# Two decoder layers on one core: the norm of queries and keys is cut into token blocks, and the steps of the attention chains are spaced anew

## The chip, the cores and the metric

The kernel runs on one core of a Trainium2 chip. The metric is the device time of one execution in microseconds, the median over runs. Five engines work side by side, each in the order of its own queue: TensorE (PE in the profile; its weight loads stand apart as PEld), VectorE (DVE), ScalarE (ACT), GpSimd (POOL) and SyncE (SP), which here issues nearly all DMAs. An instruction that has to wait holds up everything behind it in its queue.

## The reference

Input are 256 tokens of 2048 numbers, in float32. Two layers follow each other, each a mixer and an MLP around one residual stream:

```python
h = rms_norm(x, mix_norm_g[i])
x = x + (fox_attention(h, ...) if i == 0 else dilated_attention(h, ...))
h = rms_norm(x, mlp_norm_g[i])
x = x + (relu(h @ w_up) ** 2) @ w_down          # 2048 -> 8192 -> 2048
```

FoX attention (layer 0) has 16 heads of 128. One matrix gives queries, keys, values and a forget gate; queries and keys are normed per head (`q * rsqrt(mean(q*q) + eps) * gain`); the logits get the difference of the gate's cumulative log-sigmoid and a causal mask; softmax, product with the values, output matrix.

Dilated attention (layer 1) has 8 heads whose values are 256 wide, shared by three groups of dilations 1, 4 and 16. Each group has its own queries and keys, normed in the same way, a distance bias and a window; the three groups share one softmax denominator.

## The kernel before, in words

**Float32 by halves.** Every float32 operand is cut into a high half in the fast matmul format and a low half, the remainder. A product of 128 rows (`product_steps`, lines 369 to 371) is three matmuls for each of two token blocks: high x high, high x low, low x high. So each weight block of 256 rows x 512 columns, loaded by SP into `raw` (line 315), is split by `split`: ScalarE casts `wh` (L334), VectorE subtracts `wl` (L335). There are five buffers of `raw` and five of `wh` and `wl`. Each new load waits until the block just split has been read.

**Steps.** Products of 16 row blocks (`KC`) by 512 columns follow each other in a fixed order: four groups of query, key and value columns for FoX, its output matrix, the first MLP, four groups for the dilated layer (three times queries and keys, then values), its output matrix, the second MLP. One row block is one step: six matmuls, then `jobs.tick()`. At odd steps a weight block is used up and the next is split.

**Jobs.** Everything else is written as Python generators that run between the steps. `yield 3` means: go on three steps later; `yield ("fk", j)` means: go on when that key is done. This is settled while the program is built, by counting steps, not on the chip. From step 24 on `pin` fixes the order of each engine's instructions as written, so a job that is set one step later stands behind that step's work in every queue.

**The jobs that the change touches.** `qk_chain` (L544) norms the queries and keys of one product: ScalarE squares both token blocks of the accumulators (L550), VectorE sums (L554), GpSimd takes the power -0.5 (L557); three steps later VectorE multiplies by it (L563, `qn`) and turns 32x32 blocks (L572) for both token blocks in one go, and SP writes them to a scratch in DRAM (`blocks`, through `move`, L291); four steps later SP reads them back turned; six steps later ScalarE applies the gains and casts (L589, L596), and VectorE takes the low halves (L600). `transposed_by_dma` (L459) does the same for the normed input of an MLP or of the dilated layer: transpose (L466), block writes, 3 steps, read-back, 6 steps, scaling (L485, L487).

`fox_head` and `dil_head` then take the scores (`scores`, L680 and L683, into the two banks of `ps_sc`), maximum, exponential and sum, turn the probabilities by way of DRAM (`p_turned`), cast and cut them (`p_split`: `pTh` L657, two steps on `pTl` L660) and multiply them with the values (`pv`, L630 and L631). `pv` casts the result (`oTfh`, `oTdh`, L633) and takes the low half (`oTfl`, `oTdl`, L635) for the output matrix.

`in_group` runs the first three chunks of the output matrix as one group: rows 0 to 11 of all chunks first, then rows 12 to 15 of each, since the last heads come late (`CUT = 12`). When a chunk is done, `add_chain` adds it to the residual (L876) and starts the norm of that chunk. The first two chunks of an up-projection and the first two products of the dilated layer are grouped in the same way.

Tiles live in pools by tag; `bufs` says how many of a tag exist. The tag `w` holds the squares, the normed queries and keys, and the turned inputs; `sd` the three score blocks of a dilated head; `vw` a value block; `pTh` and `pTl` the probabilities.

Of the kernel before, what the change touches and what calls it, by code (L numbers as in the profile page):

```python
# [9 lines left out]
F32 = mybir.dt.float32  # L10
F32R = mybir.dt.float32r
I32 = mybir.dt.int32
AF = mybir.ActivationFunctionType
# [4 lines left out]
P = 128  # L18
# [20 lines left out]
CUT = 12  # L39
# [52 lines left out]
def trunk(ctx: ExitStack, tc, x, fox_w_in, fox_b_f, fox_q_gain, fox_k_gain, fox_w_out, dil_w_in,  # L92
# [3 lines left out]
    pinned = {"last": None}  # L96

# [146 lines left out]
    def add_group(*chunks):  # L244

        for rows in ((0, CUT * P), (CUT * P, D)):
            for w, cols in chunks:
                add(w, rows, cols)

    def add_out(w):  # L250
        add_group(*((w, [(n * NC, NC)]) for n in range(3)))
        for n in range(3, NX):
            add(w, (0, D), [(n * NC, NC)])
# [34 lines left out]
    def move(dst, src):  # L288

        with behind(issued["load"]):  # L290
            return nc.sync.dma_start(dst, src)  # L291
# [167 lines left out]
    def transposed_by_dma(tag, col, n):  # L459


        tiles = []
        for t in range(NT):
            tile_ = work.tile([P, NC], F32, tag="w", name=f"turned_{tag}_{n}_{t}", bufs=5)
            blocks = dram.tile([4, 32, 4, P], F32, tag="blocks", name=f"blocks_{tag}_{n}_{t}", bufs=4)
            nc.vector.transpose(tile_.rearrange("p (j b r) -> p b j r", j=4, b=4),  # L466
                                xt[n][:, t, :].rearrange("p (b j c) -> p b j c", j=4, c=32))
            for i in range(4):
                move(blocks[:, :, i, :].rearrange("j c x -> c j x"),
                     tile_[32 * i:32 * i + 32].rearrange("p (j x) -> p j x", j=4))  # L470
            tiles.append((tile_, blocks))
        yield 3
        for tile_, blocks in tiles:
            move(tile_, blocks.rearrange("j c i x -> (j c) (i x)"))
        yield 6
        for half in range(2):
            pr = n * 2 + half
            both = act.tile([P, 2, 2, S], F32R, tag="hT", name=f"hT_{tag}_{pr}", bufs=KC // 2)
            for i in range(2):
                gc = gain[:, col + pr * 2 + i:col + pr * 2 + i + 1]  # L480
                for t in range(NT):
                    src = tiles[t][0].rearrange("p (i b r) -> p b i r", i=4, b=4)[:, half * 2 + i]
                    hi, lo = (both[:, i, x, t * P:(t + 1) * P].rearrange("p (i r) -> p i r", i=4) for x in range(2))
                    with behind(issued["cast"]):
                        on_act = nc.scalar.activation(hi, src, AF.Copy, scale=gc)  # L485
                    with behind(issued["cut"]):
                        on_dve = nc.vector.scalar_tensor_tensor(lo, src, gc, hi.bitcast(F32), ALU.mult, ALU.subtract)  # L487
            issued[tag, pr] = issued[tag] = on_act, on_dve
            hT[tag][pr] = both
            jobs.done.add((tag, pr))  # L490
            yield 1

    def norm_chain(tag, col, n, ssp, wait, later):
# [24 lines left out]
        with behind(issued["cast"]):  # L518
            for t in range(NT):
                junk = work.tile([P, 3 * 3 * P], F32, tag="sd", name=f"junk_{tag}_{n}_{t}", bufs=1)  # L520
                nc.scalar.activation(junk[:, 0:NC], xt[n][:, t, :], AF.Square, accum_out=ssp[:, t, n:n + 1])
# [22 lines left out]
    def qk_chain(acc, tag, key, parts):  # L544
# [3 lines left out]
        for t in range(NT):  # L548
            s = work.tile([P, NC], F32, tag="w", name=f"sq_{key}_{t}", bufs=5)
            nc.scalar.activation(halves(s), by_column(acc[t]), AF.Square, scale=rstd[tag][:, t:t + 1])  # L550
            sq.append(s)
# [6 lines left out]
        yield 3  # L558
        qn = []
        for t in range(NT):  # L560
            nc.vector.tensor_scalar_mul(rq[:, t, :], rq[:, t, :], rstd[tag][:, t:t + 1])
            q = work.tile([P, 4, P], F32, tag="w", name=f"qn_{key}_{t}", bufs=5)
            nc.vector.tensor_mul(q.rearrange("p (h g) d -> p h g d", h=2),  # L563
                                 acc[t].rearrange("p (g d h) -> p h g d", h=2, g=2),
                                 rq[:, t, :].rearrange("p (h g) -> p h g", h=2).unsqueeze(3).to_broadcast([P, 2, 2, P]))
            qn.append(q)


        turns = []
        for t in range(NT):  # L570
            turned = sq[t].rearrange("p (j h r) -> p j h r", j=4, h=4)
            nc.vector.transpose(turned.rearrange("p j h r -> p h j r"),  # L572
                                qn[t].rearrange("p h (j c) -> p h j c", c=32))
# [47 lines left out]
    def pv(pt_sb, vt, cols, o_hi, o_lo, name):  # L621
        for i, c in enumerate(cols):
# [11 lines left out]
            yield 1  # L634
# [3 lines left out]
    def p_turned(p, name, landing):  # L638
# [58 lines left out]
    def gate_chain(tag, pf):  # L697
# [45 lines left out]
        yield 2  # L743
# [9 lines left out]
    def fox_head(j, hh, qT, kT, vt):  # L753
        h = 4 * j + hh
        at = ((3, 8, 13, 17) if j == 3 else (3, 9, 21, 27))[hh]
# [39 lines left out]
        yield 1 if j == 3 else 2  # L795
# [4 lines left out]
        yield from pv(pt_sb, vt, [hh * P], [hi[:, h % 2, :]], [lo[:, h % 2, :]], f"f{h}")  # L800
# [3 lines left out]
    def dil_head(q4, i, qTs, kTs, vt):  # L804
# [37 lines left out]
        yield from pv(pt_sb, vt, [i * S, i * S + P], [hi[:, 0, :], hi[:, 1, :]], [lo[:, 0, :], lo[:, 1, :]], f"d{h}")  # L842
# [49 lines left out]
    def out_proj(keys, lhs, then=None, ready=None, scale=None, group=0):  # L892
        posts = [lambda acc, n=n: add_chain(acc, n, then, ready, scale) for n in range(NX)]
        if group:
            in_group(lambda n: sums(*(() if n < 2 else (ps_tp, "tp"))),
                     lambda acc, ks: product_steps(acc, keys, lhs, ks), posts[0:group])
# [9 lines left out]
    def up_chain(banks, key, n, aT):  # L906
# [3 lines left out]
        for half in range(2):  # L910
            t = work.tile([P, 2, S], F32, tag="w", name=f"z_{key}_{n}_{half}", bufs=5)
# [82 lines left out]
    for j in range(4):  # L994
# [13 lines left out]
        for hh in range(4):  # L1008
# [5 lines left out]
             normed("n1", MLP_G, lambda n: 6 if n == 2 else 2), group=3)  # L1014
# [5 lines left out]
             normed("n3", MLP_G + KC, lambda n: 6 if n == 2 else 2), group=3)  # L1020
# [32 lines left out]
```

## Time and profile before

| | |
|---|---|
| median of 3 runs | 2206.24 us (2205.82 to 2207.99) |
| profiled execution | 2206.94 us |
| its span, first to last instruction | 2205.2 us |
| TensorE busy | 2152.4 us (98%) |
| TensorE weight loads | 1911.1 us (87%) |
| VectorE busy | 1423.7 us (65%) |
| ScalarE busy | 1095.2 us (50%) |
| GpSimd busy | 45.9 us (2%) |
| mean granted TensorE clock | 0.994 of full speed |
| read from HBM, written | 446.35 MB, 23.62 MB |

The sum of a view's busy times is no path: matmuls overlap in the pipeline, and an engine may be busy with work that nobody waits for yet. What counts is when TensorE has nothing to do, and whose work then ends its idle time. In a row of the waits, "PE po_f L630 <- DVE pTl_f L660: 15.7, 11, 1.8" reads: TensorE's matmul of line 630 that writes `po_f` waited for VectorE's instruction of line 660 that writes `pTl_f`, 15.7 us in total, 11 times, 1.8 us at the longest. "<-" means "waits for" there; within an instruction it means "is computed from".

### The profile page before, as it was taken

How to read it: one execution, taken by the hardware profiler on the slowest of the kernel's cores; microseconds unless marked ns; L12 is line 12 of the kernel's file. 1: busy time of each engine (PE TensorE's matmuls, PEld its weight loads, DVE VectorE, ACT ScalarE, POOL GpSimd, SP SyncE). 2: the span in 40 equal slices, each digit the busy share in tenths (PEclk: the TensorE clock that was granted, in tenths of full speed). 3: DMA queues.
4: the chain of work that ended last, by engine and by line, in shares of the span. 5: the costliest groups of instructions: out<-in, count | busy, mean ns of one | idle time of the engine just before them, and what ended most of it. 6: DMA issues, size and time to landing. Idle time of an engine off the chain costs nothing.

```text
span 2205.2 us, 29959 instructions
## 1 busy us (share of the span) xinstructions
PE 2152.4 (98%) x11120; PEld 1911.1 (87%) x11120; DVE 1423.7 (65%) x1893; ACT 1095.2 (50%) x1521; POOL 45.9 (2%) x40
## 2 busy tenths in 40 slices
PE   9999999999999999999998989999999999999998
PEld 7888888998998998998887878888988988988988
DVE  6678776685565565566667677767665665665663
ACT  6555554654454454445554545555544444444442
POOL 0000000000000000000010000000000000000000
PEclk9999999999999999999999999999999999999999
DMA  7778876756666656667766666767766666666663
GB/s 241 236 241 231 257 237 213 240 204 216 201 201 206 201 195 209 201 196 246 244 216 208 222 213 210 216 228 234 238 202 202 200 203 205 200 202 203 200 212 131
DMA packets 314532, 471.98 MB, mean 214 GB/s; under 512 B 36424, under 2 KB 124048, under 8 KB 314384
## 3 DMA queue, kind: packets, MB, share of 16 engines
q1 hardware_dynamic: 313792, 469.38, 67.4%
q8 instruction: 87, 1.43, 0.3%
q10 hardware_dynamic: 560, 0.66, 0.1%
q14 instruction: 61, 0.50, 0.1%
q0 software_dynamic: 32, 0.02, 0.0%
HBM read 446.35 MB, written 23.62 MB: 213 GB/s over the span
## 4 chain that ended last, share of the span: by engine, by line
PE 83%; DVE 6%; DMA 5%; ACT 2%; issue 2%; SPq 1%; POOL 1%; ACTq 0%; DVEq 0%; POOLq 0%
PE acc L369 16%; PE acc L371 16%; PE acc L370 16%; PE up_n1a_acc L433 5%; PE up_n3a_acc L433 5%; DVE wl L335 3%; DMA raw<-in_dil_w_in_dram 3%; PE up_n1a_sc L433 3%; PE up_n3a_sc L433 3%; PE up_n1a_tp L433 3%; PE up_n3a_tp L433 3%; PE up_n3a_acc L437 3%; PE up_n1a_acc L437 3%; ACT wh L334 2%; PE up_n3a_tp L437 1%
## 5 line engine op out<-in xcount | busy, mean ns | idle before, releaser
L335 DVE TENSOR_TENSOR wl<-raw,wh 128x1024 fp32r<-128x1024 f32 (+1 forms) x801 | 968.5, 1221 | 669.8 <-ACT wh L334 657.0
L334 ACT CAST wh<-raw 128x1024 fp32r<-128x1024 f32 (+1 forms) x801 | 829.6, 1047 | 841.3 <-PE acc L371 552.2
L369 PE MATMUL acc<-wh,hT_n 128*128 128x512 f32 x896 | 346.0, 387 | 0.0
L370 PE MATMUL acc<-wl,hT_n 128*128 128x512 f32 x896 | 343.2, 383 | 1.0 <-DVE wl L335 0.8
L371 PE MATMUL acc<-wh,hT_n 128*128 128x512 f32 x896 | 342.7, 383 | 0.0
L369 PE MATMUL acc<-wh,aTh_n1a 128*128 128x512 f32 x512 | 194.0, 379 | 0.0
L370 PE MATMUL acc<-wl,aTh_n1a 128*128 128x512 f32 x512 | 194.0, 379 | 0.0
L371 PE MATMUL acc<-wh,aTl_n1a 128*128 128x512 f32 x512 | 194.0, 379 | 0.0
L370 PEld LDWEIGHTS acc<-wl,hT_n 128*128 128x128 f32 x896 | 171.8, 192 | 25.0 <-DVE wl L335 2.0
L371 PEld LDWEIGHTS acc<-wh,hT_n 128*128 128x128 f32 x896 | 171.3, 191 | 25.0 <-DVE hT_n L511 0.2
L369 PEld LDWEIGHTS acc<-wh,hT_n 128*128 128x128 f32 x896 | 171.5, 192 | 23.6 <-ACT wh L334 0.4
L369 PE MATMUL acc<-wh,aTh_n3a 128*128 128x512 f32 x480 | 181.9, 379 | 0.0
L370 PE MATMUL acc<-wl,aTh_n3a 128*128 128x512 f32 x480 | 181.9, 379 | 0.0
L371 PE MATMUL acc<-wh,aTl_n3a 128*128 128x512 f32 x480 | 181.9, 379 | 0.0
L433 PE MATMUL up_n3a_acc<-hT_n,wh 128*128 128x512 f32 x512 | 181.6, 382 | 0.0
L433 PE MATMUL up_n1a_acc<-hT_n,wh 128*128 128x512 f32 x512 | 181.6, 382 | 0.0
L437 PE MATMUL up_n1a_acc<-hT_n,wl 128*128 128x256 f32 x512 | 139.6, 273 | 0.0
L437 PE MATMUL up_n3a_acc<-hT_n,wl 128*128 128x256 f32 x512 | 139.6, 273 | 0.0
L371 PEld LDWEIGHTS acc<-wh,aTl_n1a 128*128 128x128 f32 x512 | 96.8, 189 | 13.8
L370 PEld LDWEIGHTS acc<-wl,aTh_n1a 128*128 128x128 f32 x512 | 96.8, 189 | 13.8
L369 PEld LDWEIGHTS acc<-wh,aTh_n1a 128*128 128x128 f32 x512 | 96.8, 189 | 13.6
L433 PEld LDWEIGHTS up_n3a_acc<-hT_n,wh 128*128 128x128 f32 x512 | 96.8, 189 | 13.5
(673 smaller groups left out, 3166.3 us busy)
## 6 DMA issues: line engine op xcount, KB each, us to landing
raw<-in_mlp_w_up_dram SPq DMA_DIRECT2D x256, 512.0 KB, 4.6
raw<-in_mlp_w_down_dram SPq DMA_DIRECT2D x256, 512.0 KB, 4.6
raw<-in_dil_w_in_dram SPq DMA_DIRECT2D x192, 256.0 KB, 3.3
raw<-in_fox_w_in_dram SPq DMA_DIRECT2D x95, 512.0 KB, 4.6
raw<-in_fox_w_out_dram SPq DMA_DIRECT2D x32, 512.0 KB, 4.6
raw<-in_dil_w_in_dram SPq DMA_DIRECT2D x32, 512.0 KB, 3.8
raw<-in_dil_w_out_dram SPq DMA_DIRECT2D x32, 512.0 KB, 4.0
blocks_n<-turned_n SPq DMA_DIRECT2D x96, 64.0 KB, 3.5
```

The source lines that it names most:

```text
L334: issued["cast"] = nc.scalar.copy(hi[:, part, :], raw[:, part, :])
L335: issued["cut"] = nc.vector.tensor_sub(lo[:, part, :], raw[:, part, :], hi[:, part, :].bitcast(F32))
L369: nc.tensor.matmul(acc[t], ah[:, tok], hi, start=first, stop=False)
L370: nc.tensor.matmul(acc[t], ah[:, tok], lo, start=False, stop=False)
L371: issued["product"] = nc.tensor.matmul(acc[t], al[:, tok], hi, start=False, stop=last)
L433: issued["product"] = nc.tensor.matmul(banks[b], hi[:, i, col], in_turn(tokens.rearrange("p x s -> p (x s)"), P // 2), start=first, stop=last)
L437: nc.tensor.matmul(banks[b][:, 0:S], lo[:, i, col], in_turn(tokens[:, 0, :], P // 2), start=False, stop=False)
```

## The change

Seven edits, all in the order of the work; the number of instructions of every engine stays the same.

1. `qk_chain`: the multiplication waits 4 steps instead of 3, and then the two token blocks are normed, turned and written two steps apart. The read-backs are issued three steps after the second block's start, the second of them two steps after the first.
2. A new helper `clear(n)` waits n steps, or n+1, so that the job goes on at an odd step: the weights were split at the end of the odd step before, and none since. It is used where ScalarE takes up queries and keys, and probabilities, after their read-back.
3. Heads: the starts of the four FoX heads move (for instance 3, 9, 21, 27 to 3, 8, 18, 22); in the dilated layer's first three groups the turned probabilities are left 10 steps instead of 6; between the low half of the probabilities and the product with the values lie 3 steps instead of 2 in most heads, and 2 instead of 1 in the last FoX group; in the last groups the low half of the result is taken in the same step as the high half.
4. The first group of the output matrices takes its rows in three parts (0 to 11, 12 and 13, 14 and 15) instead of two; the weights are loaded in that order.
5. The read-back of a normed input is left 9 steps for the first chunk and 11 for the others, instead of 6; the added delay of 6 instead of 2 steps for the third chunk goes. In the two MLPs' inputs the third chunk's turned block lies in the tag `sd`.
6. The transpose of the gate's cumulative sum comes 4 steps after it instead of 2.
7. Buffers: `w` has 6 instead of 5, `pTh` and `pTl` have 1 instead of 2, the scratch of the sums of squares moves from `sd` to `vw`.

```diff
-CUT = 12
+PARTS = ((0, 12), (12, 16))
+OUT_PARTS = ((0, 12), (12, 14), (14, 16))
...
+    def clear(steps):
+
+        return steps + (jobs.now + steps + 1) % 2
...
-    def in_group(new, steps, posts):
+    def in_group(new, steps, posts, parts=PARTS):
...
-        for n in range(len(posts)):
-            banks.append(new(n))
-            steps(banks[n], range(CUT))
-        for n in range(len(posts)):
-            steps(banks[n], range(CUT, KC))
-            jobs.spawn(posts[n](banks[n]))
+        for a, b in parts:
+            for n, post in enumerate(posts):
+                if a == 0:
+                    banks.append(new(n))
+                steps(banks[n], range(a, b))
+                if b == KC:
+                    jobs.spawn(post(banks[n]))
...
-            tile_ = work.tile([P, NC], F32, tag="w", name=f"turned_{tag}_{n}_{t}", bufs=5)
+            if tag != "n2" and n == 2:
+
+                if t == 0:
+                    both = work.tile([P, 3, 3 * P], F32, tag="sd", name=f"turned_{tag}_{n}", bufs=1)
+                tile_ = both.rearrange("p a b -> p (a b)")[:, t * NC:(t + 1) * NC]
+            else:
+                tile_ = work.tile([P, NC], F32, tag="w", name=f"turned_{tag}_{n}_{t}", bufs=6)
...
-        yield 6
+        yield 11 if n else 9
...
-        yield 3
-        qn = []
+        yield 4
+        qn, turns = [], []
         for t in range(NT):
             nc.vector.tensor_scalar_mul(rq[:, t, :], rq[:, t, :], rstd[tag][:, t:t + 1])
...
-            qn.append(q)
-        turns = []
-        for t in range(NT):
             turned = sq[t].rearrange("p (j h r) -> p j h r", j=4, h=4)
...
+            qn.append(q)
             turns.append(blocks)
-        yield 4
-        for t in range(NT):
+            yield 2
+        yield 1
+        for t in range(NT):
+            yield 2 * t
             move(qn[t], turns[t].rearrange("j c i x -> (j c) (i x)").rearrange("p (h d) -> p h d", h=4))
-        yield 6
+        yield clear(6)
...
-            yield 1
+            yield apart
             nc.vector.tensor_sub(lo, by_token(po), hi.bitcast(F32))
...
-        yield landing
+        yield clear(landing)
         return turned
...
-        p_hi, p_lo = (work.tile([P, S], F32R, tag=f"pT{x}", name=f"pT{x}_{name}", bufs=2) for x in "hl")
+        p_hi, p_lo = (work.tile([P, S], F32R, tag=f"pT{x}", name=f"pT{x}_{name}", bufs=1) for x in "hl")
...
         nc.vector.tensor_copy(c_q, pc)
-        yield 2
+        yield 4
...
-        at = ((3, 8, 13, 17) if j == 3 else (3, 9, 21, 27))[hh]
+        at = ((2, 7, 12, 16) if j == 3 else (3, 8, 18, 22))[hh]
...
-        yield 1 if j == 3 else 2
+        yield 2 if j == 3 or hh == 3 else 3
...
-        turned = yield from p_turned(p, f"d{h}", 6)
+        turned = yield from p_turned(p, f"d{h}", 6 if q4 == 3 else 10)
         yield ("dv", q4)
         pt_sb = yield from p_split(turned, f"d{h}")
-        yield 2
+        yield 2 if q4 == 3 else 3
...
-             normed("n1", MLP_G, lambda n: 6 if n == 2 else 2), group=3)
+             normed("n1", MLP_G), group=3)
```

More of the change, by code (lines that the diff above doesn't have):

```diff
@@ L242, in add, with add_group @@
             plan.append((w, r, cols))
-    def add_group(*chunks):
-        for rows in ((0, CUT * P), (CUT * P, D)):
+    def add_group(*chunks, parts=PARTS):
+        for a, b in parts:
             for w, cols in chunks:
-                add(w, rows, cols)
+                add(w, (a * P, b * P), cols)
     def add_out(w):
-        add_group(*((w, [(n * NC, NC)]) for n in range(3)))
+        add_group(*((w, [(n * NC, NC)]) for n in range(3)), parts=OUT_PARTS)
         for n in range(3, NX):
@@ L548, in qk_chain @@
         for t in range(NT):
-            s = work.tile([P, NC], F32, tag="w", name=f"sq_{key}_{t}", bufs=5)
+            s = work.tile([P, NC], F32, tag="w", name=f"sq_{key}_{t}", bufs=6)
             nc.scalar.activation(halves(s), by_column(acc[t]), AF.Square, scale=rstd[tag][:, t:t + 1])
@@ L619, in by_token, with pv @@
         return po[:, 0:S].rearrange("p (n b) -> p b n", b=2)
-    def pv(pt_sb, vt, cols, o_hi, o_lo, name):
+    def pv(pt_sb, vt, cols, o_hi, o_lo, name, apart):
         for i, c in enumerate(cols):
@@ L799, in fox_head @@
         hi, lo = oT["f", h // 2]
[L800 removed]
+        yield from pv(pt_sb, vt, [hh * P], [hi[:, h % 2, :]], [lo[:, h % 2, :]], f"f{h}", int(j < 3))
         jobs.done.add(("of", h))
@@ L895, in out_proj @@
             in_group(lambda n: sums(*(() if n < 2 else (ps_tp, "tp"))),
-                     lambda acc, ks: product_steps(acc, keys, lhs, ks), posts[0:group])
+                     lambda acc, ks: product_steps(acc, keys, lhs, ks), posts[0:group], OUT_PARTS)
         for n in range(group, NX):
@@ L910, in up_chain @@
         for half in range(2):
-            t = work.tile([P, 2, S], F32, tag="w", name=f"z_{key}_{n}_{half}", bufs=5)
+            t = work.tile([P, 2, S], F32, tag="w", name=f"z_{key}_{n}_{half}", bufs=6)
             for i in range(2):
@@ L1019, in trunk @@
              lambda k: (oT["d", k // 2][0][:, k % 2, :], oT["d", k // 2][1][:, k % 2, :]),
-             normed("n3", MLP_G + KC, lambda n: 6 if n == 2 else 2), group=3)
+             normed("n3", MLP_G + KC), group=3)
     mlp("n3", ready=store)
```

12 lines of the change are left out of this document (6 added, 6 removed).

## The prediction

> **What bounds the kernel now.** I read the page's first lines, then busy time by stage, then who TensorE waits for, then the granted clock after the long waits, then the engines that TensorE waits for. First the page: TensorE is busy for all but some 53 us.
>
> ```profile
> span 2205.2 us, 29959 instructions
> PE 2152.4 (98%) x11120; PEld 1911.1 (87%) x11120; DVE 1423.7 (65%) x1893; ACT 1095.2 (50%) x1521; POOL 45.9 (2%) x40
> ```
>
> Busy time by stretch (stretch, its length, then busy us and instructions of PE, PEld, DVE, ACT and POOL, the granted clock, DMA share, GB/s): FoX layer with its output product, first MLP, dilated layer, second MLP.
>
> ```profile
> 25.00:375.00 350.00, 330.48 (x1611) 287.06 (x1610) 256.77 (x449) 192.46 (x317) 18.08 (x9) 1.00 0.76 232
> 375.00:1150.00 775.00, 775.00 (x4087) 693.39 (x4086) 489.68 (x591) 379.68 (x508) 6.10 (x6) 1.00 0.67 214
> 1150.00:1500.00 350.00, 326.81 (x1565) 285.30 (x1564) 242.18 (x353) 186.35 (x270) 18.43 (x10) 0.97 0.68 214
> 1500.00:2175.00 675.00, 675.00 (x3624) 605.79 (x3623) 413.93 (x466) 319.12 (x404) 0.70 (x1) 1.00 0.66 210
> ```
>
> In both MLPs TensorE has no gap at all: nothing there can be gained, only lost. The two attention stages leave 19.5 and 23.2 us idle. The waits of TensorE name nearly all of it (total us, times, longest):
>
> ```profile
> PE po_f L630 <- DVE pTl_f L660: 15.7, 11, 1.8
> PE po_d L630 <- DVE pTl_d L660: 13.3, 6, 3.3
> PE sc_d L680 <- DVE sd L817: 7.9, 1, 7.9
> PE sc_f L683 <- DVE fkT_0l L600: 2.7, 1, 2.7
> PE acc L371 <- DVE oTdl L635: 1.0, 1, 1.0
> PE acc L370 <- DVE wl L335: 0.8, 1, 0.8
> PE pct L746 <- DVE c_q L742: 0.8, 1, 0.8
> ```
>
> Sum 42.2 us, all behind VectorE. Waits also cost clock (the value after POOL's):
>
> ```profile
> 1184.70:1190.00 5.30, 5.30 (x15) 4.48 (x16) 4.54 (x6) 0.00 (x0) 0.00 (x0) 0.50 0.72 210
> 1190.00:1195.30 5.30, 5.30 (x28) 4.70 (x28) 2.05 (x2) 4.45 (x9) 0.00 (x0) 0.99 0.96 297
> 1231.00:1235.00 4.00, 4.00 (x14) 3.23 (x13) 3.93 (x8) 1.04 (x1) 0.30 (x1) 0.57 0.43 139
> 1306.00:1309.30 3.30, 3.30 (x11) 2.73 (x11) 3.23 (x7) 0.49 (x2) 1.15 (x1) 0.52 0.52 145
> 1388.00:1391.30 3.30, 3.30 (x10) 2.58 (x9) 0.28 (x1) 1.36 (x2) 0.00 (x0) 0.51 0.88 231
> ```
>
> After the 7.9 us wait, 15 matmuls stand where the next equal stretch has 28: 13 x 5.30/28 = 2.5 us. The same happens at 1231, 1306 and 1388, each just after a wait at po_d; 3.30 us at 0.51 loses 1.6, so some 5 us for the three. What can be gained in the two stages is 42.2 + 2.5 + 5 = 49.7 us.
>
> [...] The trace has halvings after waits of at most 3.3 us and none after FoX's 1.8. [...]
>
> **The change part by part.** It adds and removes no instruction; it moves steps. A step is one row block of a product, six matmuls; two steps are the distance of two weight casts:
>
> ```profile
> 362.31 1.05 ACT L334 CAST wh<-raw 128x1024 fp32r<-128x1024 f32 x1 [1.54 <-PE acc L371]
> 364.90 1.05 ACT L334 CAST wh<-raw 128x1024 fp32r<-128x1024 f32 x1 [1.54 <-PE acc L371]
> L335 DVE TENSOR_TENSOR wl<-raw,wh 128x1024 fp32r<-128x1024 f32 (+1 forms) x801 | 968.5, 1221 | 669.8 <-ACT wh L334 657.0
> ```
>
> So a step is 1.295 us. Weights are split once in two steps, and VectorE's half (1.22 us) stands ready only when the cast, 1.05 us into the next step, is done; what is queued behind it starts 2.3 us into that step.
>
> *Norm of queries and keys.* VectorE's queue before one wait in FoX:
>
> ```profile
> 114.79 0.23 DVE L561 TENSOR_SCALAR rq_('fq', 1)_1152<-rq_('fq', 1)_1152,rstd_n 128x4 f32<-128x4 f32 x1 [1.53 <-POOL rq_('fq', 1)_1152 L557]
> ...
> 117.16 0.67 DVE L572 STREAM_TRANSPOSE sq_('fq', 1)_1_1146<-qn_('fq', 1)_1_1188 128x512 f32<-128x512 f32 x1
> 117.75 1.18 DVE L335 TENSOR_TENSOR wl<-raw,wh 128x1024 fp32r<-128x1024 f32 x1
> 118.85 0.55 DVE L766 TENSOR_TENSOR bias<-bias,mask 128x384 f32<-128x384 f32 x1
> 119.32 0.42 DVE L660 TENSOR_TENSOR pTl_f<-turned_f,pTh_f 128x256 fp32r<-128x256 f32 x1
> 119.79 0.38 PE L630 MATMUL po_f<-pTl_f,fv0h 128*128 128x256 f32 x1 [1.77 <-DVE pTl_f L660]
> ```
>
> VectorE stands 1.53 us for GpSimd's power, then norms and turns both token blocks in one run (114.79 to 117.75, 2.96 us); the low half of the probabilities comes last and TensorE loses 1.77. With the yield of 4 the power lies under the next weight split, so the 1.53 goes; the run becomes two of 1.48, two steps apart; and the values' matmuls come three steps after the low half is issued, not two (FoX's first three groups except each fourth head; the dilated layer's first three groups), in FoX's last group two, not one. Counting from the step of the first block, in the new order: weights until 2.3; block one 3.8; bias .47, 4.25; weights 5.4; block two 6.9; then the next head's biased scores and maxima:
>
> ```profile
> 102.47 0.74 DVE L780 SCALAR_TENSOR_TENSOR s_f<-sc_f,c_q,bias 128x128 f32<-128x128 f32 x2
> 103.12 0.60 DVE L783 TENSOR_REDUCE nm_f<-s_f 128x1 f32<-128x128 f32 x2
> ```
>
> 1.25, 8.2; weights 9.4; low half 9.8. The values' matmul stands eight steps on, at 10.3. What was 1.77 late is .5 early. The rows are of one head, so I leave 0 to 1.8 per wait and take .3 for twelve FoX heads (3.6), .3 for eight dilated pairs (2.4). All po waits and their clock then go but for 6.0.
>
> *The read-back of queries and keys.* ScalarE waits for it at the head of its queue, with the weight casts and the next squares behind:
>
> ```profile
> ACT dqT_0w L589 <- DMA qn_('dqk', 0, 0)_0_10065<-ks_('dqk', 0, 0)_0_10071: 3.2, 1, 3.2
> ACT dqT_1w L589 <- DMA qn_('dqk', 0, 1)_0_10259<-ks_('dqk', 0, 1)_0_10265: 6.7, 1, 6.7
> ACT dqT_2w L589 <- DMA qn_('dqk', 0, 2)_0_10474<-ks_('dqk', 0, 2)_0_10480: 10.4, 1, 10.4
> ACT fkT_0w L589 <- DMA qn_('fk', 0)_0_770<-blocks_('fk', 0)_0_776: 4.9, 1, 4.9
> ```
>
> It grows by 3.6 a product: chains start 16 steps apart, ScalarE stops at step 13, so each stop delays the next chain's squares, and the third ends in the 7.9 us at the scores. In the new order ScalarE gets there at 4+2+2+1+2x0+6 and one for parity, with no stop before, 17 steps: 4 steps (5.2 us) more for the chain, and the next squares (16) now stand ahead of the stop, so it isn't inherited. From the first block's transpose it is 13 steps against 10, 3.9 us more against a growth of 3.6. On SP the eight block writes become four and four with a weight load between, and the second read-back goes behind another load, two steps later and needed two steps later. I take the 7.9 + 2.5, the 2.7 and the .8 of the weights as gone, and 2.0 of new stops reaching TensorE (0 to 3.6 of one stop).
>
> *Gate.* The cumulative gate gets two steps more: .8 goes. *Last rows.* The rows of the last two heads are asked for four steps later in the first chunk, while these heads end three to four steps later and write their low half a step sooner: the 1.0 at oTdl goes. In FoX's last group the scores follow the keys' low half by two steps, not three: 0 to 1.3, I take 1.0.
>
> *The normed input of the MLPs.* The last rows now end two steps apart, so the adds, transposes and 24 block DMAs of three chunks fall together on SP, and the fixed wait for the read-back grows from 6 steps to 9 and 11. The new order leaves 5 steps (6.5 us) from a chunk's scaling to the first up-product's use, where it left over 8. SP's rows of before:
>
> ```profile
> 367.86 3.77 SPq L291 DMA_DIRECT2D blocks_n<-turned_n  x8
> 373.88 6.02 SPq L291 DMA_DIRECT2D blocks_n<-turned_n  x8
> 381.00 2.20 SPq L291 DMA_DIRECT2D turned_n<-blocks_n  x2
> turned_n<-blocks_n SPq DMA_DIRECT2D x24, 256.0 KB, 5.2
> ```
>
> From the first transpose the second chunk's read-back needs two sets of writes (3.8 to 6.0 each), one read issue and three loads (.5 each), a third set, its own issue (.9 to 2.2) and 5.2: 21 to 30 us, against some 24 until TensorE asks for it (21 steps, less some 3 that VectorE is behind). Cover gone, it costs 0 to 6 us in each of two places; nearer the low end, as the first set took 3.77: 1.0 each, 2.0.
>
> *Buffers.* Six w buffers instead of five, the shared scratch under other tags: nothing, since the added chain length is what fills the sixth. One buffer instead of two for the probabilities: only each fourth FoX head casts a step before the third is multiplied, and ScalarE, 55% busy there (192.46 of 350), waits some 2 us under TensorE's work; if not covered, up to 2 us in three places.
>
> **Sum.** 49.7 - 6.0 - 2.0 - 1.0 - 2.0 = 38.7 us. The profiled execution took 2206.94 (span 2205.2), so 2168.2; the median, 2206.24, is .7 lower: 2167.5.
>
> **The rivals.** *Half stays.* VectorE has the same work (256.77 and 242.18 us of 350), only in other order; where it runs behind, three steps fill as two did. Then half of the po waits with their clock (34/2 = 17) stays instead of 6.0, and the MLPs take their 6 each: 49.7 - 17 - 2 - 1 - 12 = 18, 2189. For it: the longest po_d wait is 3.3, more than the step given. Against: the waits follow runs, which are halved.
>
> *Slower: the longer chain inherits after all.* Place: the second read-back on SP, behind one more load; a chain of 17 to 19 steps now overlaps the next one of 16. If ScalarE stops by the 3.6 us that one product added before, in each of 8 FoX and 12 dilated chains, and no slack covers it, that is 72 us against 38.7: 2206.9 + 33 = 2240. It decides from 38.7/20 = 1.9 us per chain. Against: the growth has a cause, the stop ahead of the next squares, which the new order takes away; the fkT row, outside that group, stands alone.
>
> *It doesn't do what it says.* If the bubbles before the values' matmuls came from too few buffers, spacing would change nothing and the single probability buffer would bring them back: only 4 us of gate, weights and oTdl go, taken by the MLPs: 2206. The row's releaser is VectorE's low half, and VectorE runs without a gap from 114.79 to it, so no buffer is waited for. [...]
>
> **How the numbers follow.** Forecast .64 (own range 2155 to 2178), half stays .21 (2178 to 2199), no change .05, slower .08; .02 is left for still more. Forecast 2167.5. The range goes from 2155, just below all 49.7 gained (2156.5 from the median), to 2194 in the second case: with the rest of that case, no change and slower it leaves out some .18. A measurement of this kernel tells .2% (4.4 us) from no change. Faster .86, same .05, slower .09.
>
> **What would show it.** Right: po_f and po_d together below 8 us, no sc_d line in TensorE's waits, dqT waits on DMA below 4 us each, clock 1.00 from 1150 to 1460, first MLP still without a gap. Wrong: a wait of the first up-products on hT, of sc_f on fkT in the last FoX group, or dqT waits that grow from product to product.

## The result, and the profile after

The changed kernel takes 2151.15 us (2149.37 to 2152.19); the kernel before took 2206.28 us (2201.33 to 2210.99) beside it. The ratio is 0.9749, with a 95% interval of 0.9736 to 0.9762: 2.5% faster. The forecast was 2167.5 with a range from 2155 to 2194. Its direction holds; the gain is 55 us where 38.7 were forecast, and the time lies 4 us below the range.

All lines of the code behind the first edits are shifted in the changed kernel: L334, L335, L589, L600, L630, L660 and L680 of before are L340, L341, L601, L612, L642, L672 and L692 of after. The page of the profiled execution (2150.94 us), its span and busy times:

```profile
span 2149.2 us, 29907 instructions
PE 2136.6 (99%) x11120; PEld 1906.8 (89%) x11120; DVE 1425.8 (66%) x1893; ACT 1094.9 (51%) x1521; POOL 42.3 (2%) x40
```

TensorE has the same 11120 matmuls, and 12.6 us are left in which it has none, of 52.8. The busy times by stretch (columns as in the prediction; the kernel runs ahead of before, so the later stretches don't hold quite the same work):

```profile
25.00:375.00 350.00, 349.44 (x1725) 307.99 (x1724) 272.74 (x472) 206.64 (x342) 13.81 (x9) 1.00 0.80 249
375.00:1150.00 775.00, 775.00 (x4080) 694.00 (x4079) 495.38 (x596) 383.81 (x506) 9.34 (x8) 1.00 0.67 215
1150.00:1500.00 350.00, 348.12 (x1745) 308.90 (x1744) 264.72 (x389) 201.55 (x306) 15.84 (x8) 1.00 0.74 234
```

The two attention stretches, which had 19.5 and 23.2 us without a matmul, now have 0.6 and 1.9, and the clock of the second is whole (1.00, was 0.97). In the same 350 us of the dilated layer stand 1745 matmuls where 1565 stood. The MLP has no gap, as before. The waits of TensorE, all that there are:

```profile
PE spare L146 <- POOL ident masks.py:199: 2.5, 1, 2.5
PE last L418 <- DVE x L886: 2.2, 1, 2.2
PE po_d L642 <- DVE pTl_d L672: 1.9, 1, 1.9
PE ps_g_mix L165 <- DMA g_mix<-in_mix_norm_g_dram: 1.8, 1, 1.8
PE sc_f L695 <- DVE fkT_0l L612: 0.3, 1, 0.3
PE pf L706 <- DVE wfs L199: 0.2, 1, 0.2
```

Of the seven rows that the prediction added up to 42.2 us, two are left with 2.2. The other four are the start, the gate's weights and the end of the kernel, which the change doesn't touch. ScalarE's waits:

```profile
ACT pTh_f L669 <- PE po_f L642: 5.7, 3, 1.9
...
ACT hT_n L498 <- DMA turned_n<-blocks_n: 2.9, 4, 1.4
ACT sq_('dqk', 3, 0)_0_12414 L601 <- DMA qn_('dqk', 3, 0)_1_12512<-ks_('dqk', 3, 0)_1_12515: 2.7, 1, 2.7
...
ACT dqT_0w L601 <- DMA qn_('dqk', 2, 0)_0_11611<-ks_('dqk', 2, 0)_0_11614: 0.6, 1, 0.6
```

The stops at the read-back of queries and keys, which grew from 3.2 over 6.7 to 10.4 in before, are gone: over all such rows they are 3.6 us in 3 rows, where before has 38.0 in 12.

### The profile page after: what moved, and what is told of

Its sections match the earlier page's. It is cut to its first block, busy times and chain, and to the rows that moved or that the text cites. A ratio compares the mean times of both kernels' runs of the same rounds, so it can differ in the third digit from the quotient of the medians.

```text
span 2149.2 us, 29907 instructions
## 1 busy us (share of the span) xinstructions
PE 2136.6 (99%) x11120; PEld 1906.8 (89%) x11120; DVE 1425.8 (66%) x1893; ACT 1094.9 (51%) x1521; POOL 42.3 (2%) x40
## 4 chain that ended last, share of the span: by engine, by line
PE 97%; DVE 1%; ACT 1%; DMA 1%; issue 0%; SPq 0%; POOL 0%; ACTq 0%; DVEq 0%; POOLq 0%
PE acc L375 21%; PE acc L376 21%; PE acc L377 21%; PE up_n1a_acc L440 5%; PE up_n3a_acc L440 5%; PE up_n3a_sc L440 3%; PE up_n1a_tp L440 3%; PE up_n1a_sc L440 3%; PE up_n3a_tp L440 3%; PE up_n1a_acc L444 3%; PE up_n3a_acc L444 3%; PE up_n3a_sc L444 1%; PE up_n3a_tp L444 1%; PE up_n1a_sc L444 1%; PE up_n1a_tp L444 1%; DVE wl L341 0%
## 5 line engine op out<-in xcount | busy, mean ns | idle before, releaser
L341 DVE TENSOR_TENSOR wl<-raw,wh 128x1024 fp32r<-128x1024 f32 (+1 forms) x801 | 970.1, 1221 | 636.9 <-ACT wh L340 624.7
L340 ACT CAST wh<-raw 128x1024 fp32r<-128x1024 f32 (+1 forms) x801 | 830.6, 1047 | 880.3 <-PE acc L377 580.0
L376 PEld LDWEIGHTS acc<-wl,aTh_n1a 128*128 128x128 f32 x512 | 96.9, 189 | 13.7
```

The lines of the kernel that those rows point to most:

```text
L340: issued["cast"] = nc.scalar.copy(hi[:, part, :], raw[:, part, :])
L341: issued["cut"] = nc.vector.tensor_sub(lo[:, part, :], raw[:, part, :], hi[:, part, :].bitcast(F32))
L376: nc.tensor.matmul(acc[t], ah[:, tok], lo, start=False, stop=False)
```

## The experiments

Times are medians. Ratios are to the kernel before on the same chip, whose median was 2205.6 to 2207.2 there. A price is the median less the 2151.15 of the change. Prices under some 3 us say little: the medians of the kernel before alone differ by 1.6 us between the chips, and in 5 of the 14 profiles the matmuls behind the last wait of the kernel run at half clock (0.51 in before, against 1.00 in the change), which takes 1.7 us; none of the edits lies there.

**The length of the read-back chain, shortened in the changed kernel.** Theory A here is the prediction's: ScalarE's stops at the read-back carry part of the gain. The edit takes ScalarE to the data 13 steps after the product's end, as in before, instead of 17. It does not bring back the whole chain of before: the read-backs are still set at the steps 9 and 11, where before has both at 7, so by the count of steps the data have 4 and 2 steps to land instead of 6 (in the traces, the second read-back of the second dilated product goes out 15.0 us after the squares instead of 13.5). The edit:

```diff
-        yield clear(6)
+        yield clear(2)
```

> The changed kernel with the read-back of queries and keys left 2 steps instead of 6, so that ScalarE reaches it 13 steps after the squares, as before the change, with the two-block order kept. Theory A (the length of the chain is what counts: a stop before the next squares is inherited): dqT waits on DMA of 3, 7 and 10 us return in the first dilated group, and with them the wait at the dilated scores and its clock: 2151 + 8 to 20 us. Theory B (four and four block writes get the data back sooner, the length doesn't matter): within 3 us of 2151, dqT waits below 3.

2204.91 us (2199.31 to 2206.29), ratio 0.9992 (0.9983 to 1.0002). The whole gain of 55 us is gone, far more than either theory gave, although blocks, spare steps and all the rest of the change are still there. TensorE's waits in this kernel:

```profile
PE po_d L642 <- DVE pTl_d L672: 13.7, 3, 4.7
PE po_f L642 <- DVE pTl_f L672: 8.3, 5, 2.8
PE sc_f L695 <- DVE fkT_0l L612: 4.4, 3, 3.0
PE sc_d L692 <- DVE sd L829: 4.4, 2, 4.1
PE sc_f L695 <- ACT fkT_0h L608: 2.6, 1, 2.6
```

The waits of VectorE and ScalarE that belong to it, the latter for the three products of the first dilated group:

```profile
DVE wl L341 <- ACT wh L340: 689.3, 526, 8.7
```

```profile
ACT dqT_2w L601 <- DMA qn_('dqk', 0, 2)_0_10486<-ks_('dqk', 0, 2)_0_10489: 8.5, 1, 8.5
...
ACT dqT_1w L601 <- DMA qn_('dqk', 0, 1)_0_10271<-ks_('dqk', 0, 1)_0_10274: 5.2, 1, 5.2
...
ACT dqT_0w L601 <- DMA qn_('dqk', 0, 0)_0_10077<-ks_('dqk', 0, 0)_0_10080: 2.7, 1, 2.7
```

The growing row of before is back (2.7, 5.2, 8.5), and all stops of this kind add up to 84.6 us (38.0 in before). The main thing to see is the first two rows of TensorE: there are waits for the *probabilities'* low halves again, 22.0 us of them, with the added step and single blocks in place. The path runs over the row of VectorE: while ScalarE stands at the read-back, the weight cast behind it is late, VectorE stands up to 8.7 us for it, and whatever is queued behind that is late too. One such path in order of time, from ScalarE's stop over VectorE's wait for the cast to the wait of TensorE:

```profile
1389.80 0.51 ACT L601 ACTIVATE dqT_0w<-qn_('dqk', 3, 0)_0_12497,gain 128x256 f32<-128x256 f32 x1 [7.86 <-DMA qn_('dqk', 3, 0)_0_12497<-ks_('dqk', 3, 0)_0_12500]
...
1392.26 1.23 DVE L341 TENSOR_TENSOR wl<-raw,wh 128x1024 fp32r<-128x1024 f32 x1 [8.72 <-ACT wh L340]
...
1403.22 0.58 PE L642 MATMUL po_d<-pTl_d,dv2h 128*128 128x256 f32 x1 [4.75 <-DVE pTl_d L672]
```

Between the last two VectorE works off what has piled up, with one gap of 1.16 us, until it reaches the low half at 1402.78. Not every stop does this: those of 2.7 and 5.2 us above are followed by no wait of TensorE.

The rest of the loss is in large part clock. Six stretches of this kernel run at half clock, 6.83 us each (from 92.72, 290.69, 1178.16, 1229.36, 1304.45 and 1400.02 us); the mean clock is 0.98 from 25 to 375 us and 0.96 from 1150 to 1500, where the change has 1.00 in both. The sum of the six (length, then busy time of each engine):

```profile
sum 40.96, PE 28.92 PEld 24.21 DVE 37.56 ACT 7.33 POOL 0.00; mean PE 4.82 PEld 4.04 DVE 6.26 ACT 1.22 POOL 0.00
```

TensorE is busy for 28.9 us of them, and half of that, 14.5 us, is lost; the change has no such stretch before its last matmul. The five rows above are 33.4 us, less the 2.2 of after. Together 45.7 of the 50.6 us between the two spans; the waits cost more than their idle time besides, as shown further below.

**Two steps between.** The same edit with `clear(4)`, 15 steps:

```diff
-        yield clear(6)
+        yield clear(4)
```

> The changed kernel with ScalarE taking up the read-back of queries and keys 15 steps after the product's end instead of 17: between the change and the kernel with 13 steps, which lost the whole gain (2204.91). Products end 16 steps apart, so at 15 the stop still stands ahead of the next product's squares in ScalarE's queue, at 17 behind them. Theory A (the stop is inherited while it stands ahead of the next squares, and is not once it stands behind them): most of the loss is there already, 2180 to 2200 us, with stops of ScalarE that grow or stay above 3 us from product to product in the dilated layer. Theory B (only the time that the data lacks counts, and nothing is handed on): two steps are 2.6 us per stop, a single stop lacks less than that, slack in ScalarE's queue takes most of it: 2152 to 2165 us, stops below 2.6 us.

2170.27 us (2166.59 to 2173.42), ratio 0.9833 (0.9818 to 0.9848): 19 us. Neither theory has it; it lies between their ranges. TensorE's waits, then ScalarE's stops:

```profile
PE po_d L642 <- DVE pTl_d L672: 10.0, 3, 5.4
PE sc_f L695 <- DVE fkT_0l L612: 2.8, 2, 2.0
```

```profile
ACT dqT_1w L601 <- DMA qn_('dqk', 1, 1)_0_10934<-ks_('dqk', 1, 1)_0_10937: 5.9, 1, 5.9
...
ACT dqT_2w L601 <- DMA qn_('dqk', 0, 2)_0_10486<-ks_('dqk', 0, 2)_0_10489: 2.8, 1, 2.8
...
ACT dqT_0w L601 <- DMA qn_('dqk', 1, 0)_0_10680<-ks_('dqk', 1, 0)_0_10683: 2.1, 1, 2.1
...
ACT dqT_1w L601 <- DMA qn_('dqk', 0, 1)_0_10271<-ks_('dqk', 0, 1)_0_10274: 1.0, 1, 1.0
...
ACT dqT_0w L601 <- DMA qn_('dqk', 0, 0)_0_10077<-ks_('dqk', 0, 0)_0_10080: 0.3, 1, 0.3
```

The first product's stop fell from 2.7 to 0.3, by nearly the two steps (2.6 us); that part is plain latency, as theory B says. But the stops still grow from product to product (0.3, 1.0, 2.8; 2.1, 5.9), as theory A says, so something is handed on, though in smaller portions. Over all rows the stops are 28.4 us. With 84.6, 28.4 and 3.6 us of stops the kernel loses 54, 19 and nothing: between these three kernels, each microsecond that ScalarE stands costs some 0.7 us, two thirds of (84.6 - 3.6) and three quarters of (28.4 - 3.6). It is no general price. Before stands 23.0 us for the normed inputs, and TensorE has no gap in either MLP; and the kernel before with the spare step alone (below) has 61.4 us of the stops counted here, against 38.0 in before, and is 10 us faster. The runs don't show a sharp edge at the 16 steps of a product; what they show is that at 17 the data are there.

**Parts of the change in the kernel before.** The longer chain alone, in the first three dilated groups, with the change's buffers (`w` 6, probabilities 1, squares' scratch under `vw`):

```diff
-        yield 6
+        yield 10 if key[0] == "dqk" and key[1] < 3 else 6
```

> The kernel before with one thing of the change: in the dilated layer's first three groups the read-back of queries and keys is left 10 steps instead of 6, so ScalarE reaches it after 17 steps, behind the next squares (with the six w buffers that this needs, and the other buffers of the change). Both token blocks still go in one run. Theory A (length alone): the growing stops 3.2, 6.7, 10.4 go below 3, the 7.9 us wait at the scores and its 2.5 us of clock go: 2206 - 10 = 2196, range 2192 to 2200. Theory B (the cut into two blocks is needed): 2204 to 2208.

2194.38 us (2189.93 to 2196.11), ratio 0.9945 (0.9927 to 0.9963), 11 us faster, as theory A has it. The 7.9 at the scores is gone, and po_d falls from 13.3 to 10.7. The same for FoX was not run. The wait of the values' matmuls alone:

```diff
-        yield 1 if j == 3 else 2
+        yield 2 if j == 3 or hh == 3 else 3
...
-        yield 2
+        yield 2 if q4 == 3 else 3
```

> The kernel before with one thing of the change: 3 steps instead of 2 from the probabilities' low half to the product with the values, 2 instead of 1 in the last FoX group. Theory A (one step, 1.3 us, more): each of some twenty waits of about 1.8 us shrinks by 1.3, and the shortest vanish, 2206 - 15 to 25 us, and the halvings of the clock after po_d go. Theory B (VectorE is behind by as much, since the work ahead of it moves along): 2206 - 0 to 8 us.

2195.68 us (2195.26 to 2199.57), ratio 0.9958 (0.9942 to 0.9974), 10 us faster, between the two theories:

```profile
PE po_d L630 <- DVE pTl_d L660: 11.9, 6, 3.9
PE po_f L630 <- DVE pTl_f L660: 9.3, 10, 1.7
PE sc_d L680 <- DVE sd L817: 7.9, 1, 7.9
```

Ten waits in FoX stay with 9.3 of their 15.7 us, and the dilated ones hardly move. ScalarE's stops for queries and keys rise from 38.0 to 61.4 us. A spare step alone doesn't remove these waits. Both edits in one kernel:

> The kernel before with two edits that were run alone: the read-back of queries and keys left 10 steps instead of 6 in the first three dilated groups (alone 11 us faster than the kernel before) and the values' matmuls one step later (alone 10 us faster). Theory A (the two act on different waits and add): 21 us faster, 2184 to 2187 us. Theory B (a stop of ScalarE also makes VectorE's low half late, so the spare step is worth more once the stops are gone): more than the sum, 28 us or more, 2178 us or less. Theory C (both remove the same waits at the dilated values' matmuls): less than the sum, 2188 to 2193 us.

2176.15 us (2174.55 to 2176.97), ratio 0.9858 (0.9841 to 0.9874): 31 us faster, more than the 21 of the two alone. The product of the two single ratios would be 0.9903, above the interval. Theory B holds:

```profile
PE po_f L630 <- DVE pTl_f L660: 10.5, 11, 2.2
PE po_d L630 <- DVE pTl_d L660: 5.9, 4, 2.2
PE sc_f L683 <- DVE fkT_0l L600: 3.0, 1, 3.0
```

The dilated waits, 13.3 in before, are 10.7 with the one edit, 11.9 with the other and 5.9 with both: neither edit alone takes them away, and a step to spare is worth more once ScalarE's stops no longer use it up (61.4 us of them with the spare step alone, 19.3 with both). FoX, whose chain this kernel leaves short, keeps 10.5.

**The spare step, undone in the changed kernel.**

```diff
-        yield 2 if j == 3 or hh == 3 else 3
+        yield 1 if j == 3 else 2
...
-        yield 2 if q4 == 3 else 3
+        yield 2
```

> The changed kernel with the distance from the probabilities' low half to the product with the values put back: 2 steps instead of 3 in most heads, 1 instead of 2 in the last FoX group. Theory A (the extra step is what takes the waits away): by the sum of VectorE's queue the low half is done 9.8 us after the first block's step and the product would now stand at 9.0, so some .8 us and a restart of .2 come back in about twenty places: 2151 + 8 to 20 us. Theory B (the halved norm runs take them away): the low half is in time at 2 steps too, and the time stays within 3 us of 2151.

2157.99 us (2156.42 to 2160.62), ratio 0.978 (0.9766 to 0.9795): 7 us, a little under theory A, and above B. TensorE waits 3.2 us at po_d and 0.5 at po_f, so only part of the 7 is idle time. In its profile the groups of these matmuls take 6.1 us more from start to start than in the change (23.5 against 17.4), and 1.7 us are the clock behind the last wait (mean clock of the profiled execution 0.999, in the change 1.000).

**The token blocks, in one run again.** Both blocks are normed in one go at the fourth step; the first read-back is issued as late as in the change:

```diff
-            yield 2
-        yield 1
+            yield 5
```

(the new wait stands ahead of the loop over the read-backs, behind both blocks)

> The changed kernel with both token blocks normed and turned in one run at step 4; the read-backs stay at their steps. Theory A (the cut into two runs carries the gain at the values' products): po waits of 1 to 2 us return in FoX, 2151 + 8 to 20 us. Theory B (both runs lie ahead of the low half in VectorE's queue in any case, so the cut is neutral): within 3 us of 2151, po waits below 4 us in total.

2155.6 us (2152.63 to 2159.11), ratio 0.9769 (0.9754 to 0.9783): 4.5 us, between the two theories, with 3.4 us at po_f and 2.0 at po_d. Undone alone, the cut that gives the change its name costs a twelfth of the gain.

**The turned probabilities, left 6 steps again in the dilated layer.**

```diff
-        turned = yield from p_turned(p, f"d{h}", 6 if q4 == 3 else 10)
+        turned = yield from p_turned(p, f"d{h}", 6)
```

> The changed kernel with the turned probabilities of the first three dilated groups left 6 steps instead of 10 (the more steps to values). Theory A (the product with the values then stands right behind the norm run of the next keys): po_d waits of 2 to 3 us return in about six heads with some clock, 2151 + 8 to 18 us. Theory B (the third step before the product is enough): within 3 us of 2151.

2160.14 us (2157.6 to 2164.78), ratio 0.9795 (0.9773 to 0.9817): 9 us, theory A. TensorE's wait and ScalarE's stop:

```profile
PE po_d L642 <- DVE pTl_d L672: 8.0, 4, 3.0
```

```profile
ACT pTh_d L669 <- DMA turned_d<-pblocks_d: 13.7, 6, 3.6
```

It is the same pattern as in the chain: six stops of ScalarE, 13.7 us, and 9 us lost. In before, with the same six steps, this stop was only 0.4 us. My reading: there ScalarE was late at the heads already and their data had time to land; with ScalarE on time, six steps are too few. The kernel before with the longer chain alone fits it: there the stop is 7.0 us.

**The normed input of the MLPs.**

```diff
-        yield 11 if n else 9
+        yield 6
```

> The changed kernel with the read-back of the normed inputs left 6 steps again instead of 9 and 11. Theory A (ScalarE and VectorE have room there): ScalarE's waits for the read-back grow to 20 us or more, TensorE has no wait in the MLPs, within 2 us of 2151. Theory B (the stop of ScalarE blocks the weight casts until TensorE runs dry): 2151 + 3 to 12 us, waits at the first up-products or at the out-projection before them.

2158.31 us (2155.89 to 2160.01), ratio 0.9784 (0.9768 to 0.9799): 7 us, theory B.

```profile
PE up_n1a_sc L444 <- DVE wl L341: 2.6, 2, 1.8
...
PE up_n1a_tp L444 <- DVE wl L341: 2.1, 1, 2.1
...
PE up_n3a_sc L444 <- DVE wl L341: 1.8, 1, 1.8
```

ScalarE stands 32.4 us for this read-back (longest 8.8), the casts behind it are late, and the first up-products of both MLPs wait for the weights' low half, not for their input. With 9 and 11 steps the stops are 2.9 us and neither wait exists.

**Three small parts.** The output matrix's rows in two parts:

```diff
-OUT_PARTS = ((0, 12), (12, 14), (14, 16))
+OUT_PARTS = PARTS
```

> The changed kernel with the output matrices' first group in two parts again (rows 12 to 15 of each chunk together), so that the last two heads are asked for four steps sooner, while the heads still end late. Theory A: TensorE waits for the last head in both layers, by one product with the values, a cast and a low half, some 2 us in FoX and 2 to 4 us in the dilated layer, 2151 + 3 to 7 us. Theory B (other work covers it): within 2 us.

2152.68 us (2151.6 to 2153.17), ratio 0.9754 (0.9738 to 0.977): 1.5 us, theory B; its profiled execution has the half clock at the end (mean 0.999). The multiplication three steps after the squares:

```diff
-        yield 4
+        yield 3
```

> The changed kernel with the multiplication of the norm three steps after the squares instead of four (the chain is one step shorter, and its last wait is made up to an odd step again). Theory A (the prediction's: VectorE then stands up to 1.5 us for GpSimd's power, and what is queued behind it, the low half of the probabilities, is late): the waits at the values' matmuls come back by 2 to 6 us, 2154 to 2158 us, and VectorE waits for GpSimd's power some 1.5 us in most of 20 chains. Theory B (the two single blocks with the spaced steps leave room for that stand): within 2 us of the change, whatever VectorE waits.

2153.65 us (2152.15 to 2156.64), ratio 0.976 (0.9745 to 0.9774): 2.5 us, with an interval that overlaps the change's. VectorE stands for GpSimd's power in 7 of the 20 chains (0.7 to 1.8 us; in 1 with the change), not in most, and TensorE waits 3.8 us at po_f. This is between the two theories. The helper for odd steps, without parity:

```diff
-        return steps + (jobs.now + steps + 1) % 2
+        return steps
```

> The changed kernel with the helper for odd steps returning the plain number of steps, so that ScalarE takes up queries, keys and probabilities in whatever step it comes, also in those in which a weight block is cast. Theory A (a take-up in a step with a weight split delays the cast or is delayed by it, and VectorE's half behind it): 2155 to 2162 us, new waits of TensorE at the accumulators for the low half of weights or at the values' matmuls. Theory B (parity is nothing; only the number of steps counts, and that falls by one at most): 2150 to 2155 us.

2153.17 us (2151.71 to 2154.34), ratio 0.9756 (0.9741 to 0.977): theory B. Taking up data at an odd step is worth 2 us, if anything: the interval overlaps the change's.

## Why the prediction was right and wrong

*Right.* Every sign that it named for its own case is there: po_f and po_d together 1.9 (below 8), no wait at sc_d, no dqT stop on a DMA above 0.6 (below 4), a whole clock, no gap in the first MLP. Of the signs against it one came, and only at 0.3 us: the scores of the last FoX group wait for their keys, for which it had set aside 1.0. What it called the cause of the 7.9 us, a stop ahead of the next squares that each product hands on, was borne out by the kernel with 13 steps, which brings the growing stops back. The single buffer for probabilities makes ScalarE wait for TensorE three times, 5.7 us in all, for nothing lost: two microseconds in three places, as it said.

*Wrong: the terms were taken as independent.* The prediction gave each wait one cause and one price: halved runs and a spare step for the values' matmuls, the chain's length for the 7.9 + 2.5, the 2.7 and the .8. For before its reading of VectorE's queue holds in FoX. In the stretch from 100 to 360 us, in which all eleven po_f waits lie (15.7 us), ScalarE stops for queries and keys only 2.4 us:

```profile
ACT fkT_0w L589 <- DMA qn_('fk', 1)_0_1445<-blocks_('fk', 1)_0_1451: 1.0, 1, 1.0
ACT fkT_0w L589 <- DMA qn_('fk', 2)_0_2141<-blocks_('fk', 2)_0_2147: 0.7, 1, 0.7
ACT fkT_0w L589 <- DMA qn_('fk', 3)_0_2837<-blocks_('fk', 3)_0_2843: 0.7, 1, 0.7
```

The changed kernel with 13 steps has 21.3 us of these stops in the same stretch, and 8.3 us at po_f, 7.7 of them in three waits behind a stop. So the stops did not make FoX wait in before; they come when other waits go (38.0 us in before, 61.4 with the spare step, 84.6 with all of the change but the chain's length), and then bring waits at the values' matmuls of their own. That the data have less time to land once TensorE no longer waits is the likely reason; no run tests it by itself. The prediction priced the chain's length by the stops that before shows, some 14 us. Added to before in three dilated groups it brings 11, taken from the change it costs 54. The prices of the parts undone (54, 9, 7, 7, 4.5, 2.5, 2, 1.5) add up to some 87 us, well above the 55 of them all. The heads' new starts, the gate's two steps and the earlier low half of the last results were not run alone.

*Wrong: what was left over.* "49.7 - 6.0 - 2.0 - 1.0 - 2.0" kept 11 us in the kernel: 6.0 at the values' matmuls, 2.0 for new stops, 1.0 for FoX's last scores, 2.0 for the MLPs' input. Left are 1.9, nothing, 0.3 and nothing. That is 8.8 us of the 17 by which the gain was underrated. The .3 per head, near the low end of 0 to 1.8, was an allowance for the heads whose rows had not been added up. No head of FoX used it; the 1.9 us that are left stand behind one stop of ScalarE, the row of 2.7 us above.

*Wrong: the ceiling.* The 49.7 us were taken as all that there is, and the range ended "just below all 49.7 gained". The span fell by 56.0. Two things were not in it. First, a wait costs more than the idle time in its row. In before the matmuls around the wait of 1.77 us start here, and below them stands the first matmul after the last wait of the kernel:

```profile
117.74 0.27 PE L630 MATMUL po_f<-pTh_f,fv0h 128*128 128x256 f32 x1
...
120.26 0.46 PE L369 MATMUL acc<-wh,hT_n 128*128 128x512 f32 x1
...
2179.81 0.44 PE L411 MATMUL last<-wh,aTh_n3a 128*128 128x256 f32 x1 [2.17 <-DVE x L874]
```

and in after, where the first group has no wait:

```profile
120.87 0.27 PE L642 MATMUL po_f<-pTh_f,fv0h 128*128 128x256 f32 x1
...
121.34 0.46 PE L375 MATMUL acc<-wh,hT_n 128*128 128x512 f32 x1
...
2125.47 0.35 PE L418 MATMUL last<-wh,aTh_n3a 128*128 128x256 f32 x1 [2.17 <-DVE x L886]
```

The group takes 2.52 us with the wait (117.74 to 120.26) and 0.47 without (120.87 to 121.34): 2.05 us are lost where the row says 1.77. The record of the group's first matmul lasts 0.27 us in both, but in after the next ones start every 0.11 (120.87, 120.98, 121.09), so the overlap of the first two is lost with the wait as well. Over all po_f and po_d groups the distances from start to start shrank from 49.8 to 17.4 us, by 32.4, where the idle time shrank by 27.1; 5.3 us of the error are this. Second, the end of the kernel: 1.7 us, which no edit accounts for. Both kernels wait 2.17 us there (the third rows above), but the matmuls behind the wait run at a clock of 0.51 in before and of 1.00 in after. The stretches after it, of before and of after:

```profile
2179.90:2183.30 3.40, 3.40 (x13) 3.13 (x14) 0.42 (x1) 0.03 (x1) 0.00 (x0) 0.51 0.41 154
```

```profile
2125.60:2129.00 3.40, 3.40 (x24) 3.19 (x25) 0.91 (x2) 1.05 (x1) 0.00 (x0) 1.00 0.41 154
```

8.8 + 5.3 + 1.7 make 15.8 of the 17.3 us between 56.0 and 38.7; no row accounts for the other 1.5. So the steps that put the number off are the terms left over and the ceiling. The dependence between the parts, which it also missed, doesn't explain the number: the change has the longer chain and the spare step together, as the sum assumed.

Two of its figures do not come out of their own terms, and neither enters the 38.7. "4+2+2+1+2x0+6 and one for parity" make 16, not 17; the program's steps make 17 without the one, since two more lie ahead of the second read-back. And gate, weights and oTdl, .8 + .8 + 1.0, make 2.6, not 4.

*The rivals.* "Half stays" named 17 us at the values' matmuls and 12 in the MLPs; 1.9 and nothing came. That 6 steps would be too few for the MLPs' input was a sound worry: with them 7 us are lost, and the 9 and 11 steps prevent it. "The longer chain inherits after all" has the dependence the wrong way round: the short chain is the one that hands on. "It doesn't do what it says" fell with the rows of the waits; what the single buffer costs without the rest was not tried.

## What to carry to other kernels

Where one in-order queue both casts what the critical engine eats and waits for data from a DMA, a stop at its head can reach the critical engine under the names of engines and tiles that stand two queues away. What it costs depends on the slack around it: here from nothing (before's normed inputs) over 7 us for 32.4 us of stops to 54 us for 84.6. So follow a frequent wait back through every queue until it ends at a DMA or at the start of a chain, and expect stops at read-backs to grow when another wait is taken away: the longer chain and the spare step brought 11 and 10 us alone and 31 together. A part that brings little by itself may be what holds the others up, so undo it in the changed kernel too. And price a wait by the distance between starts, with and without it, not by its idle time alone.

## What the runs showed of the hardware

In these traces the clock after a wait isn't settled by the wait's length alone: the same 2.17 us at the end of both kernels were followed by 13 matmuls at a clock of 0.51 in one and by 24 at 1.00 in the other, over 3.40 us each. Before shows the same within one execution. Three of its waits, and 3.40 us behind each of them (behind the second from 1231.00 us, where the clock falls):

```profile
91.69 0.38 PE L683 MATMUL sc_f<-fkT_0l,fqT_0h 128*128 128x256 f32 x1 [2.72 <-DVE fkT_0l L600]
...
1229.86 0.38 PE L630 MATMUL po_d<-pTl_d,dv0h 128*128 128x256 f32 x1 [1.93 <-DVE pTl_d L660]
...
1290.64 0.38 PE L630 MATMUL po_d<-pTl_d,dv1h 128*128 128x256 f32 x1 [2.56 <-DVE pTl_d L660]
```

```profile
91.70:95.10 3.40, 3.40 (x17) 3.02 (x18) 3.40 (x6) 1.69 (x3) 0.00 (x0) 1.00 0.61 163
1231.00:1234.40 3.40, 3.40 (x10) 2.72 (x9) 3.33 (x7) 1.04 (x1) 0.30 (x1) 0.50 0.45 150
1290.70:1294.10 3.40, 3.40 (x19) 3.08 (x20) 1.35 (x2) 1.42 (x2) 0.00 (x0) 1.00 0.86 234
```

The shortest of the three, 1.93 us, is followed by half clock; those of 2.56 and 2.72 us are not. In before the matmuls behind the waits of 2.17, 2.55, 3.33 and 7.94 us (at 2179.81, 1387.20, 1305.71 and 1184.68 us) run at half clock too, and those behind FoX's waits at po_f, at most 1.77 us, at the whole. What decides it was not shown, so in this kernel what a single wait of 2 or 3 us costs in clock can't be told from its length.

With many such waits the clock is a large part of the price: in the kernel with 13 steps 14.5 of the 50.6 us between the spans, against the prediction's 7.5 of 49.7 us for before.
